# Seven-product column pairs in the branch gates and the output projection, with a group's late work spread over the next group and operands made chunk by chunk

## The chip, the cores and the metric

The kernel runs on one core of a Trainium2 chip. The metric is the device time of one execution in microseconds (us), given as the median of several runs. All data are float32; a weight or an activation is split into a rounded float32r part ("high") and the remainder ("low"), and a product is made of three matmuls: high times high, low times high, high times low.

## The reference, cut to what matters

One layer of a hybrid block for 256 rows of width 4096. Every matrix product below has 256 rows on the left.

```
xn   = rms_norm(x, norm_in_g)
proj = xn @ w_in                      # 4096 -> q, k, v, z_a, a_c, g_c, z_c, each 2048 wide
y_a  = rms_norm(attention(q, k, v), attn_out_g) * silu(z_a)
y_c  = rms_norm(conv_module(a_c, g_c), conv_out_g) * silu(z_c)
h    = x + concat(y_a, y_c) @ w_out   # 4096 x 4096
gate = sigmoid(rms_norm(h, ple_norm_g) @ w_ple_gate + b_ple_gate)   # 4096 x 4096
h    = h + gate * (p @ w_ple)         # 256 x 4096
out  = rms_norm(h, final_g)
```

The norms' row factors are applied after the products; their column gains go into the left operand.

## The kernel before, in words

**Left operands.** A 256 x 512 chunk of activations is turned by TensorE (`transposed`, L142: eight transposes of 128 x 128) and split into high and low (`split_from_psum`, L132: ScalarE writes the high part at L136, VectorE the low part at L137) into one tile `big_t` for four contraction blocks of 128. The operands of the products are `xT` (of x, eight tiles), `yT` (of the gated branches) and `hT` (of h).

**Plain products.** `product` (L206) makes 256 x 512 results: for each pair of contraction blocks it loads a 512 KB weight tile `wt` on SyncE's queue, ScalarE casts it to `wh` (L188), VectorE makes the remainder `wl` (L189), and TensorE does 12 matmuls (2 blocks x 2 row halves x 3 kinds) into two PSUM banks. A full chunk of 512 columns has 192 matmuls. After each weight tile `fill(2)` takes two pieces of postponed work from the list `later`.

**Seven-product units.** `mixed_product` (L276) makes 256 x 1024 results. One unit is two contraction blocks, that is 2 x 2 blocks of the left operand and 2 x 2 of the weights. A plain unit does the eight block products, 24 matmuls. A starred unit does seven (a Strassen-Winograd scheme), 21 matmuls: it needs four sums of left blocks, made once by `combine` (L253, tiles `hS`) and two sum tiles of weights, `ua` and `ub`, which VectorE makes for each unit in four additions of 512 columns (L330 to L335). In a starred unit VectorE makes two remainders of 1024 columns for `ua` and `ub`, one of 1024 for the second weight tile and one of 512 for the first, beside these four additions; in a plain unit it makes two remainders of 1024. A starred unit uses four more PSUM banks, the helpers `P1`, `P5`, `P6`, `P7`, which share the pool of the transposes. The order of the 16 units of a group is a string; a star marks a seven-product unit. The groups of before have 7 starred and 9 plain units, 7 x 21 + 9 x 24 = 363 matmuls in place of 384.

**The stages after attention**, in the order of the work:

- the convolution's pointwise product (`w_pw`, L710);
- the branch gates: `gated` (L721), eight plain chunks of `w_in`; after each chunk silu on ScalarE (L725) and one multiplication for each row half on VectorE (L726), then `to_operand` (the chunks of the attention at once, those of the convolution after the last gate);
- the output projection (L751): eight plain chunks of `w_out`; after each, the residual sum (L758), the square sums (L759), the operand `hT` and its sums `hS` for one pair of blocks in four;
- the embedding gates (L850): chunks 0 to 5 of `w_ple_gate` as three groups of `mixed_product`, here called E1, E2, E3. `add_gated_pair` (L813) follows each group: the sums of the helpers (L820 to L828), two small products with `w_ple`, and for each of four quarters the last sum (L837), the sigmoid (L838), three VectorE steps (L839, L840, L842) and a square sum on ScalarE (L841);
- chunks 6 and 7 as plain products, then the final norm.

**What sets the order.** A scheduler arranges each engine's instructions from the program's order; each engine then works through its list strictly in that order, and so do SyncE's DMA issues. Pools bound how far an engine can run ahead: five weight tiles `wt`, three each of `wh` and `wl`, two each of `uh` and `ul`, four PSUM banks for results and four for transposes or helpers.

Of the kernel before, what the change touches and what calls it, by code (L numbers as in the profile page):

```python
# [26 lines left out]
def hybrid_block(  # L27
# [113 lines left out]

    def transposed(src, blocks, then=lambda ins: None):  # L142

        pt = tmp_psum()
        for i, b in enumerate(blocks):
            for h in range(NH):
                then(
                    nc.tensor.transpose(  # L148
                        pt[:, i * T + h * P : i * T + (h + 1) * P],
                        src[:, h, b * P : (b + 1) * P],  # L150
                        ident,
                    )
                )
        return [pt[:, i * T : (i + 1) * T] for i in range(len(blocks))]
# [51 lines left out]
    def product(w, col, lhs, kblocks, pool=None, tag="acc", ahead=None, lag=(), given=()):  # L206
# [9 lines left out]
        for k0 in starts:  # L216
# [18 lines left out]
            fill(2)  # L235
# [17 lines left out]
    def combine(dst, at, pts, g):  # L253
# [9 lines left out]
        stt(s5, pts[1][:, P:], g[:, 1:2], a10, ALU.mult, ALU.subtract)  # L263
        stt(s2, s5, -1.0, a00, ALU.mult, ALU.subtract)
        stt(s4, pts[1][:, :P], g[:, 1:2], s2, ALU.mult, ALU.add)
# [3 lines left out]
        nc.vector.tensor_tensor(lo, src, hi.bitcast(F32), ALU.subtract)  # L269

# [5 lines left out]
    def mixed_product(w, col, lhs, comb, order, after=None):  # L276
# [25 lines left out]

        for n, (pair, seven) in enumerate(order):
            wts = []
# [16 lines left out]
            if not helper:  # L321
# [17 lines left out]
            def s_of(i):  # L339
                t, at = comb(pair)  # L340
# [378 lines left out]


    def gated(y, col, r_y):  # L721
        acc = product(w_in0, col, xT, KD)
        sz = spool.tile([P, NH, NB], F32, tag="stage", name="sz")
        for h in range(NH):
            nc.scalar.activation(sz[:, h, :], acc[h], AF.Silu, scale=r_x[:, h : h + 1])  # L725
            nc.vector.scalar_tensor_tensor(  # L726
                y[:, h, :], y[:, h, :], r_y[:, h : h + 1], sz[:, h, :], ALU.mult, ALU.mult
            )

    def to_operand(y, g, c):  # L730
# [3 lines left out]
    yT = []
    for c, y in enumerate(y_a):
        gated(y, o_za + c * NB, r_a)
        to_operand(y, ga, c)
    for c, y in enumerate(y_c):
        gated(y, o_zc + c * NB, r_c)
    for c, y in enumerate(y_c):  # L740
        to_operand(y, gc, c)


    hs, hT, hS = [], [], []
    last_transpose = []

    def hT_last(ins):
        last_transpose[:] = [ins]

    ssq_h = cpool.tile([P, NH, D // NB], F32, name="ssq_h")  # L750
    for c in range(D // NB):  # L751
        hc = act.tile([P, NH, NB], F32, tag="act", name="hc")
        nc.sync.dma_start(
            hc, x[0, :, c * NB : (c + 1) * NB].rearrange("(h q) n -> q h n", q=P)
        )
        acc = product(w_out[0], c * NB, yT, KD)
        for h in range(NH):
            nc.vector.tensor_tensor(hc[:, h, :], acc[h], hc[:, h, :], ALU.add)  # L758
            square_sum(ssq_h[:, h, c : c + 1], hc[:, h, :])  # L759
        t = big_tile()  # L760
        if c % 2 == 0:
            hS.append(big_tile())
        for pair in range(2):
            blocks = (2 * pair, 2 * pair + 1)
            pts = transposed(hc, blocks, then=hT_last)
            for b, pt in zip(blocks, pts):
                split_from_psum(t, b, pt, gp[:, 4 * c + b : 4 * c + b + 1])
            if pair == 0 and c < D // NB - 1:
                combine(hS[c // 2], 2 * (c % 2), pts, gp[:, 4 * c : 4 * c + 2])
        hs.append(hc)  # L770
        hT.append(t)
# [3 lines left out]
    pin = spool.tile([P, NH, PLE], F32, tag="stage", name="pin")  # L775
    nc.sync.dma_start(pin, p[0, 0].rearrange("(h q) n -> q h n", q=P))
    pT = spool.tile([P, PLE // P, 2, T], F32R, tag="pT_in", name="pT_in", bufs=1)
    ppt = tmp_psum()
    for b in range(PLE // P):
        for h in range(NH):  # L780
            nc.tensor.transpose(
                ppt[:, b * T + h * P : b * T + (h + 1) * P], pin[:, h, b * P : (b + 1) * P], ident
            )
        split_from_psum(pT, b, ppt[:, b * T : (b + 1) * T], 1.0)
# [28 lines left out]
    def add_gated_pair(c0, c, helper):  # L813
# [97 lines left out]
```

## Time and profile before

| | us |
|---|---|
| median of the 3 runs shown | 2111.97 (2111.31 to 2112.86) |
| the profiled execution, whole | 2111.11 |
| its span, first to last instruction | 2109.1 |
| TensorE busy (matmuls) | 2086.6 |
| VectorE busy | 1388.8 |
| ScalarE busy | 999.3 |
| GpSimd busy | 37.6 |
| mean granted TensorE clock | 0.997 |

The profiled execution took 2.0 us more than its span and 0.9 us less than the median. Matmuls are pipelined: each is shown for 0.39 us but the next begins after 0.23 us, so a busy share says when TensorE had something to do, and the number of matmuls in a stretch says how fast it went. An idle time in brackets stands ahead of an instruction with what released it. Stretches of a window view can be cut at any time; here they are cut at the first matmul of a group.

### The profile page before, as it was taken

What the parts mean: (1) busy time and instruction counts of PE and PEld (TensorE: products, weight loads), DVE (VectorE), ACT (ScalarE), POOL (GpSimd) and SP (SyncE); (2) the same over time, 40 slices, a digit from 0 to 9 for tenths busy, and PEclk for the clock granted to TensorE, in tenths of its full rate; (3) what the DMA queues carried; (4) which work ended last, traced back from release to release, by engine and by line L of the source; (5) the groups of instructions that cost most, each with busy time, mean ns of one, the idle gap of its engine ahead of it and who ended that gap; (6) DMA issues with size and microseconds to landing.
All of it is one profiled execution on the core that took longest, in us unless ns stands there. A gap on an engine that the chain in (4) does not pass through costs nothing.

```text
span 2109.1 us, 25226 instructions
## 1 busy us (share of the span) xinstructions
PE 2086.6 (99%) x9386; PEld 1717.3 (81%) x9386; DVE 1388.8 (66%) x1817; ACT 999.3 (47%) x1256; POOL 37.6 (2%) x38
## 2 busy tenths in 40 slices
PE   9999999999999999999999999999999999999997
PEld 7888888888888888888888888888888888787886
DVE  5599965498548956765455444465544479999854
ACT  7444445444544444654444444454444465555544
POOL 0000000000000002200000000000000000000000
PEclk9999999999999999999999999999999999999999
DMA  8666666666666665656666666676666666666664
GB/s 287 189 190 190 189 191 179 191 188 190 180 190 189 190 199 162 187 173 208 193 200 206 200 191 196 197 219 189 190 190 190 191 195 202 198 215 213 210 206 168
DMA packets 203092, 412.23 MB, mean 195 GB/s; under 512 B 13006, under 2 KB 16222, under 8 KB 202970
## 3 DMA queue, kind: packets, MB, share of 16 engines
q1 hardware_dynamic: 202682, 410.11, 63.9%
q8 instruction: 73, 1.20, 0.2%
q10 hardware_dynamic: 288, 0.52, 0.1%
q14 instruction: 49, 0.40, 0.1%
HBM read 406.39 MB, written 4.19 MB: 195 GB/s over the span
## 4 chain that ended last, share of the span: by engine, by line
PE 96%; DVE 2%; DMA 1%; issue 1%; ACT 0%; POOL 0%; SPq 0%; ACTq 0%; POOLq 0%; DVEq 0%
PE acc L201 82%; PE acc L292 9%; PE acc_P L292 3%; PE tmp_ps L148 1%; DMA xin<-in_x_dram 1%; DVE wl L189 1%; PE tmp_ps L616 0%; PE tmp_ps L631 0%; PE tmp_ps L649 0%; DVE z L839 0%; DMA wt<-in_w_ple_gate_dram 0%; PE tmp_ps L655 0%; PE tmp_ps L656 0%; PE tmp_ps L630 0%; ACT wh L188 0%
## 5 line engine op out<-in xcount | busy, mean ns | idle before, releaser
L201 PE MATMUL acc<-wh,big_t 128*128 128x512 f32 x5088 | 1585.9, 392 | 0.1
L189 DVE TENSOR_TENSOR wl<-wt,wh 128x1024 fp32r<-128x1024 f32 (+1 forms) x741 | 901.7, 1220 | 628.0 <-ACT wh L188 625.4
L188 ACT CAST wh<-wt 128x1024 fp32r<-128x1024 f32 (+1 forms) x741 | 768.2, 1039 | 961.4 <-PE acc L201 855.7
L201 PEld LDWEIGHTS acc<-wh,big_t 128*128 128x128 f32 x5088 | 954.3, 188 | 195.0 <-DVE big_t L137 0.7
L201 PE MATMUL acc<-wl,big_t 128*128 128x512 f32 x2544 | 992.3, 390 | 0.6 <-DVE wl L189 0.5
L201 PEld LDWEIGHTS acc<-wl,big_t 128*128 128x128 f32 x2544 | 478.2, 188 | 99.3 <-DVE wl L189 1.7
L467 DVE SCALAR_TENSOR_TENSOR cv<-uT,dw,cv 128x256 f32<-128x256 f32 x480 | 202.1, 478 | 0.5
L292 PE MATMUL acc<-wh,big_t 128*128 128x512 f32 x516 | 158.9, 391 | 0.0
L292 PEld LDWEIGHTS acc<-wh,big_t 128*128 128x128 f32 x516 | 97.3, 189 | 20.8 <-ACT wh L188 0.4
L292 PE MATMUL acc<-wl,big_t 128*128 128x512 f32 x258 | 98.7, 394 | 3.6 <-DVE wl L189 3.6
L292 PEld LDWEIGHTS acc<-wl,big_t 128*128 128x128 f32 x258 | 48.7, 190 | 14.5 <-DVE wl L189 4.4
L292 PE MATMUL acc_P<-uh,big_t 128*128 128x512 f32 x126 | 38.5, 391 | 0.0
L188 ACT CAST uh<-ub 128x1024 fp32r<-128x1024 f32 x21 | 22.1, 1052 | 29.1 <-DVE ub L335 23.9
L137 DVE SCALAR_TENSOR_TENSOR big_t<-tmp_ps,prm,big_t 128x256 fp32r<-128x256 f32 x64 | 27.8, 477 | 2.6 <-ACT big_t L136 2.4
L136 ACT ACTIVATE big_t<-tmp_ps,prm 128x256 fp32r<-128x256 f32 x64 | 26.9, 471 | 5.4 <-DVE big_t L137 5.3
L292 PEld LDWEIGHTS acc_P<-uh,big_t 128*128 128x128 f32 x126 | 23.3, 188 | 5.6 <-ACT uh L188 1.1
L189 DVE TENSOR_TENSOR ul<-ub,uh 128x1024 fp32r<-128x1024 f32 x21 | 25.6, 1219 | 3.5 <-ACT uh L188 3.5
L188 ACT CAST uh<-ua 128x1024 fp32r<-128x1024 f32 x21 | 22.1, 1051 | 10.9 <-DVE ua L331 10.2
L189 DVE TENSOR_TENSOR ul<-ua,uh 128x1024 fp32r<-128x1024 f32 x21 | 25.6, 1219 | 1.5 <-ACT uh L188 1.5
L362 ACT ACTIVATE junk<-hc 128x512 bf16<-128x512 f32 x32 | 19.9, 623 | 11.1 <-DVE hc L840 6.0
L292 PE MATMUL acc_P<-ul,big_t 128*128 128x512 f32 x63 | 24.0, 392 | 0.0
L330 DVE TENSOR_TENSOR ua<-wt 128x512 f32<-128x512 f32 x21 | 14.4, 688 | 12.1 <-DMA wt<-in_w_ple_gate_dram 12.0
(176 smaller groups left out, 766.3 us busy)
## 6 DMA issues: line engine op xcount, KB each, us to landing
wt<-in_w_in_dram SPq DMA_DIRECT2D x447, 512.0 KB, 3.9
wt<-in_w_out_dram SPq DMA_DIRECT2D x128, 512.0 KB, 3.7
wt<-in_w_ple_gate_dram SPq DMA_DIRECT2D x128, 512.0 KB, 4.1
wt<-in_w_pw_dram SPq DMA_DIRECT2D x32, 512.0 KB, 4.5
hc<-in_x_dram SPq DMA_DIRECT2D x8, 512.0 KB, 4.9
wt<-in_w_ple_dram SPq DMA_DIRECT2D x8, 512.0 KB, 4.9
out_dram<-hc SPq DMA_DIRECT2D x16, 256.0 KB, 2.9
xin<-in_x_dram SPq DMA_DIRECT2D x7, 512.0 KB, 8.4
```

Of the source, the lines that this page charges most:

```text
L136: nc.scalar.activation(hi, src, AF.Identity, scale=scale),
L137: nc.vector.scalar_tensor_tensor(lo, src, scale, hi.bitcast(F32), ALU.mult, ALU.subtract),
L148: nc.tensor.transpose(pt[:, i * T + h * P : i * T + (h + 1) * P], src[:, h, b * P : (b + 1) * P], ident,)
L188: nc.scalar.copy(wh[:, :kc, :], wt[:, :kc, :]),
L189: nc.vector.tensor_tensor(wl[:, :kc, :], wt[:, :kc, :], wh[:, :kc, :].bitcast(F32), ALU.subtract),
L201: nc.tensor.matmul(acc, a, b[:, k, :], start=kb == 0 and kind == 0, stop=kb == kblocks - 1 and kind == 2,)
L292: nc.tensor.matmul(banks[name], a, b, start=name not in begun, stop=final and ends[name] == n and kind == 2,)
L330: plus(ua[:, 0], w0[:, 0], w0[:, 1])
L362: nc.scalar.activation(junk, src, AF.Square, accum_out=dst)
L467: nc.vector.scalar_tensor_tensor(cv[:, i, :], uT[:, i, k : k + T], dw[:, b, k : k + 1], cv[:, i, :], ALU.mult, ALU.add,)
```

## The change

- The branch gates become four groups of `mixed_product` (here G1 to G4), the output projection four groups (W1 to W4). The embedding gates keep three groups (E1 to E3) and two plain chunks.
- Three orders replace two: `steady` (7 starred units) for most groups, `delayed` (5) for G1, `late` (4) for W1 and E1. Before, E1 had 7. Starred units: G 5 + 7 + 7 + 7, W 4 + 7 + 7 + 7, E 4 + 7 + 7, in all 69 against 21.
- The sums of left blocks for x (`xS`) are made from the split operand (`combine_again`); those for y and h by `combine` as before.
- `operand` makes an operand chunk with its sums; `y_ahead` and `h_ahead` call it from within W1 and E1, two chunks before the first unit and one more as the units go on, so that the operands of y and of h are made inside the first group that uses them.
- The sums of the helpers run right after the last starred unit (`on_helpers`). After a group only the four last sums and the activation are left at once; the rest (`later`) is taken two pieces per unit (four in the embedding gates) during the next group.

The core of the diff:

```diff
-    def mixed_product(w, col, lhs, comb, order, after=None):
+    steady = units("1 0* 3 2* 5 4* 7 6* 9 8* 11 10* 13 12* 15 14")
+    delayed = units("1 3 5 7 0* 9 2* 11 4* 13 6* 15 8* 10 12 14")
+    late = units("1 3 5 7 9 11 13 15 0* 2 4* 6 8* 10* 12 14")
+
+    def mixed_product(w, col, lhs, comb, order, on_helpers, ahead=None, fills=0, on_begin=None):
...
+        last_seven = max(n for n, (_, seven) in enumerate(order) if seven)
         for n, (pair, seven) in enumerate(order):
+            if ahead:
+                ahead(pair)
...
+                fill(fills)
                 continue
...
+            if n == last_seven:
+                on_helpers(helper)
+            fill(fills)
+        return c
...
+    def operand(src, g, c, tiles, combs):
+        t = big_tile()
+        if c % 2 == 0:
+            comb_tile(combs)
+        for pair in range(2):
+            blocks = (2 * pair, 2 * pair + 1)
+            pts = transposed(src, blocks)
+            for b, pt in zip(blocks, pts):
+                split_from_psum(t, b, pt, g[:, b : b + 1])
+            if pair == 0 and c < D // NB - 1:
+                combine(combs[c // 2], 2 * (c % 2), pts, g[:, :2])
+        tiles.append(t)
...
-    def gated(y, col, r_y):
-        acc = product(w_in0, col, xT, KD)
...
+    def helper_sums(helper, z):
+        z01, z10, z11 = z[0][:, 1], z[1][:, 0], z[1][:, 1]
+        nc.scalar.copy(z10, helper["P1"])
+        tt(z10, helper["P6"], z10, ALU.add)
+        tt(z01, helper["P5"], z10, ALU.add)
+        tt(z10, helper["P7"], z10, ALU.add)
+        tt(z11, helper["P5"], z10, ALU.add)
...
+    def gated(ys, c0, col, r_y, order):
+        z = sum_tiles()
+        def on_helpers(helper):
+            nc.scalar.copy(z[0][:, 0], helper["P1"])
+            helper_sums(helper, z)
+        acc = mixed_product(w_in0, col + c0 * NB, xT, xS, order, on_helpers, fills=2)
+        for h, j in ((0, 0), (1, 0), (0, 1), (1, 1)):
+            zz, y = z[h][:, j], ys[c0 + j][:, h, :]
+            tt(zz, acc[h][j], zz, ALU.subtract if j else ALU.add)
+            nc.scalar.activation(zz, zz, AF.Silu, scale=r_x[:, h : h + 1])
+            later.append(partial(stt, y, y, r_y[:, h : h + 1], zz, ALU.mult, ALU.mult))
...
-        acc = product(w_out[0], c * NB, yT, KD)
...
+        acc = mixed_product(
+            w_out[0], c0 * NB, yT, yS, steady if c0 else late, on_helpers,
+            ahead=None if c0 else y_ahead, fills=2,
+        )
+        for h, j in ((0, 0), (1, 0), (0, 1), (1, 1)):
+            hc = hs[c0 + j][:, h, :]
+            tt(hc, acc[h][j], hc, ALU.add)
+            later.append(partial(square_sum, ssq_h[:, h, c0 + j : c0 + j + 1], hc))
...
+    def gated_pair(c0, order, ahead):
...
+        todo = []
+        for h, j in ((0, 0), (1, 0), (0, 1), (1, 1)):
+            gt, hc = z[h][:, j], hs[c0 + j][:, h, :]
+            stt(gt, acc[h][j], r_h[:, h : h + 1], gt, ALU.mult, ALU.subtract if j else ALU.add)
+            nc.scalar.activation(gt, gt, AF.Sigmoid)
+            later.append(partial(tt, gt, pacc[j][h], gt, ALU.mult))
+            todo.append(partial(tt, hc, hc, gt, ALU.add))
+            todo.append(partial(square_sum, ssq_f[:, h, c0 + j : c0 + j + 1], hc))
+            todo.append(partial(tt, hc, hc, fgs[j], ALU.mult))
+        later.extend(todo)
```

How instructions move, at three places that the prediction speaks of.

VectorE, from E1 to E2, before: L837 are the four last sums, L839, L840 and L842 the late steps, `wl_13930` and `wl_13946` the remainders of E2's first unit.

```order
L837 SCALAR_TENSOR_TENSOR z_13839<-acc11_13176,r_h_13156,z_13839 128x512
L839 TENSOR_TENSOR z_13838<-acc0_13849,z_13838 128x512
L839 TENSOR_TENSOR z_13839<-acc1_13850,z_13839 128x512
L840 TENSOR_TENSOR hc_10553<-hc_10553,z_13838 128x512
L840 TENSOR_TENSOR hc_10553<-hc_10553,z_13839 128x512
L839 TENSOR_TENSOR z_13838<-acc0_13869,z_13838 128x512
L842 TENSOR_TENSOR hc_10553<-hc_10553,row_13889 128x512 x2
L840 TENSOR_TENSOR hc_10880<-hc_10880,z_13838 128x512
L839 TENSOR_TENSOR z_13839<-acc1_13870,z_13839 128x512
L189 TENSOR_TENSOR wl_13930<-wt_13925,wh_13929 128x1024
```

The same place in the change: L933 are the last sums, L171 the late steps taken from the list, `wl_14689` and `wl_14705` E2's first unit.

```order
L933 SCALAR_TENSOR_TENSOR z_13754<-acc11_13758,r_h_13748,z_13754 128x512
L192 TENSOR_TENSOR wl_14689<-wt_14684,wh_14688 128x1024
L171 TENSOR_TENSOR z_13753<-acc0_14630,z_13753 128x512
L171 TENSOR_TENSOR z_13754<-acc1_14631,z_13754 128x512
L383 TENSOR_TENSOR ua_14732<-wt_14724,wt_14726 128x512
L171 TENSOR_TENSOR z_13753<-acc0_14650,z_13753 128x512
L192 TENSOR_TENSOR wl_14705<-wt_14686,wh_14704 128x1024
L171 TENSOR_TENSOR z_13754<-acc1_14651,z_13754 128x512
L192 TENSOR_TENSOR wl_14735<-wt_14724,wh_14734 128x512
```

The first remainder of E2 stood behind nine late steps and now stands right behind the last sums, and only four late steps are left ahead of the first starred unit's remainders.

VectorE, from G2 to G3, in the change: `wl_9454` and `wl_9470` are G3's first unit, L809 the last sums of G2, L171 its late multiplications.

```order
L192 TENSOR_TENSOR wl_9454<-wt_9449,wh_9453 128x1024
L192 TENSOR_TENSOR ul_9504<-ua_9495,uh_9503 128x1024
L809 TENSOR_TENSOR z_8762<-acc00_8764,z_8762 128x512
L809 TENSOR_TENSOR z_8763<-acc10_8766,z_8763 128x512
L809 TENSOR_TENSOR z_8762<-acc01_8765,z_8762 128x512
L809 TENSOR_TENSOR z_8763<-acc11_8767,z_8763 128x512
L192 TENSOR_TENSOR wl_9470<-wt_9451,wh_9469 128x1024
L171 SCALAR_TENSOR_TENSOR y_a_6141<-y_a_6141,r_a_7401,z_8762 128x512
```

Before, two plain chunks met here, with two multiplications between remainders:

```order
L189 TENSOR_TENSOR wl_8691<-wt_8688,wh_8690 128x1024
L726 SCALAR_TENSOR_TENSOR y_a_4380<-y_a_4380,r_a_7401,sz_8644 128x512
L189 TENSOR_TENSOR wl_8709<-wt_8706,wh_8708 128x1024
L726 SCALAR_TENSOR_TENSOR y_a_4380<-y_a_4380,r_a_7401,sz_8644 128x512
L189 TENSOR_TENSOR wl_8727<-wt_8724,wh_8726 128x1024
```

The four last sums stand in one row ahead of the second remainder of the next group's first unit.

The start of W1 in the change, on TensorE: the last matmuls of G4 (into `acc11`), the transposes of two y chunks, the first matmuls of W1 on blocks of `big_t_10818`.

```order
L339 MATMUL acc11_10129<-wl_10782,big_t_528 128x512
L150 MATMUL tmp_ps_10820<-ident_96,y_a_2607 128x128 x4
L150 MATMUL tmp_ps_10838<-ident_96,y_a_2607 128x128 x4
L150 MATMUL tmp_ps_10848<-ident_96,y_a_4380 128x128 x4
L150 MATMUL tmp_ps_10866<-ident_96,y_a_4380 128x128 x4
L339 MATMUL acc00_10814<-wh_10879,big_t_10818 128x512
```

and on ScalarE, where L810 are G4's silus, L191 a cast of W1's weights, L136 the high parts of the first operand:

```order
L810 ACTIVATE z_10124<-z_10124,r_x_613 128x512
L191 CAST wh_10944<-wt_10940 128x1024
L810 ACTIVATE z_10125<-z_10125,r_x_613 128x512
L810 ACTIVATE z_10124<-z_10124,r_x_613 128x512
L810 ACTIVATE z_10125<-z_10125,r_x_613 128x512
L136 ACTIVATE big_t_10818<-tmp_ps_10820,prm_619 128x256
L136 ACTIVATE big_t_10818<-tmp_ps_10838,prm_619 128x256
```

The first operand of W1 comes right after G4's last matmul on TensorE, and behind a cast and three silus on ScalarE. Before, the chunks of the attention were turned between the gates, and plain matmuls stood between those of the convolution.

More of the change, by code (lines that the diff above doesn't have):

```diff
@@ L204, in accumulate, with product @@
             )
[L206 removed]
+    def product(w, col, lhs, kblocks, pool=None, tag="acc", ahead=None, lag=(), given=(), fills=2):
         acc = [
@@ L350, in mixed_product @@
             add("P4", block(k1, 1), (ubh[:, 1], ubl[:, 1]), n, True)
-            if after is not None and len(begun) and first >= 0 and not getattr(add, "tied", False):
+            if begins and on_begin:
+                on_begin()
+            if begins:
                 tc.add_manual_dep(
-                    made[first].ins, after.ins.name,
+                    made[first].ins, last_transpose[0].ins.name,
                     mybir.DependencyInfo(mybir.DependencyClass.NoSync, mybir.DependencyReason.DATA),
-                    reason="transposes before helpers",
+                    reason="transposes before the helpers take their banks",
                 )
-                add.tied = True
-        return c, helper
+            if n == last_seven:
+                on_helpers(helper)
+            fill(fills)
+        return c
     def square_sum(dst, src):
@@ L734, in hybrid_block @@
[L734 to L754, printed above, removed]
-        )
-        acc = product(w_out[0], c * NB, yT, KD)
[L757 to L771, printed above, removed]
@@ L772, in hybrid_block @@
-    r_h = rstd_of(ssq_h, D, "r_h")
[L775 to L784, printed above, removed]
+    tt, stt = nc.vector.tensor_tensor, nc.vector.scalar_tensor_tensor
@@ new lines, in helper_sums, with sum_tiles @@
+    def helper_sums(helper, z):
[5 more added lines that the diff above has]
+        tt(z11, helper["P5"], z10, ALU.add)
+    def sum_tiles():
+        return [spool.tile([P, 2, NB], F32, tag="stage", name="z") for _ in range(NH)]
+    xS = []
+    for c in range(D // NB - 1):
+        if c % 2 == 0:
+            comb_tile(xS)
+        combine_again(xS[c // 2], 2 * (c % 2), xT[c], 0)
@@ new lines, in hybrid_block, with y_ahead @@
+    for ys, o_z, r_y in ((y_a, o_za, r_a), (y_c, o_zc, r_c)):
+        for c0 in range(0, len(ys), 2):
+            gated(ys, c0, o_z, r_y, delayed if ys is y_a and c0 == 0 else steady)
+    fill(len(later))
+    yT, yS = [], []
+    def y_ahead(pair):
+        while len(yT) < min(pair // 2 + 2, D // NB):
+            c = len(yT)
+            y, g, at = (y_a[c], ga, 4 * c) if c < len(y_a) else (y_c[c - len(y_a)], gc, 4 * (c - len(y_a)))
+            operand(y, g[:, at : at + 4], c, yT, yS)
+    hs, hT, hS = [], [], []
@@ new lines, in hybrid_block, with embedding, h_ahead @@
+    fill(len(later))
+    r_h = rstd_of(ssq_h, D, "r_h")
+    pT = []
+    def embedding():
+        pin = spool.tile([P, NH, PLE], F32, tag="row", name="pin", bufs=3)
+        nc.sync.dma_start(pin, p[0, 0].rearrange("(h q) n -> q h n", q=P))
+        pT.append(hS[-1][:, 2:, :, :])
+        for b, pt in enumerate(transposed(pin, range(PLE // P))):
+            split_from_psum(pT[0], b, pt, 1.0)
+    def h_ahead(pair):
+        while len(hT) < min(pair // 2 + 2, D // NB):
+            c = len(hT)
+            operand(hs[c], gp[:, 4 * c : 4 * c + 4], c, hT, hS)
+            if len(hT) == D // NB:
+                embedding()
@@ L859, in hybrid_block @@
+        later.extend(todo)
+    for c0 in range(0, n_f - 2, 2):
+        gated_pair(c0, steady if c0 else late, None if c0 else h_ahead)
     for c in range(n_f - 2, n_f):
```

121 lines of the change are left out of this document (64 added, 57 removed).

## The prediction

> **What bounds the kernel now.** I read the page first, then a table of stretches, then the order of time around the slowest of them. The page's span, busy times and chain of waits:
>
> ```profile
> span 2109.1 us, 25226 instructions
> ...
> PE 2086.6 (99%) x9386; PEld 1717.3 (81%) x9386; DVE 1388.8 (66%) x1817; ACT 999.3 (47%) x1256; POOL 37.6 (2%) x38
> ...
> PE 96%; DVE 2%; DMA 1%; issue 1%; ACT 0%; POOL 0%; SPq 0%; ACTq 0%; POOLq 0%; DVEq 0%
> ```
>
> TensorE holds 96% of the chain, so a matmul removed is worth its full distance to the next one, as long as the other engines keep up. The long merged pieces of the chain give that distance, and the time of a transpose:
>
> ```profile
> 1198.93 171.41 PE acc L201 x756
> ...
> 1730.82 0.82 PE tmp_ps L148 x6
> ```
>
> 171.41 / 756 = 0.2267 us for a matmul. Next, stretches cut at the first matmul of a gate chunk, an output chunk, E1, E2, E3 and chunk 6, then a steady piece inside E2, then the start of E2. The columns are length, then busy time and count of each engine, then the clock.
>
> ```profile
> 1016.40:1059.90 43.50, 43.50 (x194) 36.03 (x193) 21.24 (x21) 18.75 (x21) 0.69 (x1) 1.00 0.66 194
> 1419.20:1462.70 43.50, 43.50 (x195) 35.79 (x193) 23.53 (x27) 19.48 (x24) 0.00 (x0) 1.00 0.64 188
> 1729.46:1818.58 89.12, 89.12 (x400) 73.62 (x399) 79.71 (x100) 52.87 (x63) 0.69 (x1) 1.00 0.64 204
> 1818.58:1912.22 93.64, 90.30 (x388) 73.21 (x387) 86.00 (x105) 52.78 (x66) 0.00 (x0) 0.98 0.62 203
> 1912.22:2004.88 92.66, 91.22 (x400) 74.39 (x399) 86.50 (x105) 52.09 (x64) 0.00 (x0) 1.00 0.65 210
> 2004.88:2049.38 44.50, 43.98 (x193) 35.88 (x192) 24.42 (x23) 18.12 (x21) 0.00 (x0) 1.00 0.71 213
> 1856.00:1876.40 20.40, 20.40 (x92) 16.89 (x91) 18.73 (x22) 12.27 (x13) 0.00 (x0) 1.00 0.63 200
> ...
> 1821.50:1826.50 5.00, 2.61 (x7) 1.79 (x8) 5.00 (x8) 2.61 (x6) 0.00 (x0) 0.80 0.28 87
> 1826.50:1830.00 3.50, 3.50 (x14) 2.81 (x13) 3.50 (x6) 0.20 (x2) 0.00 (x0) 0.80 0.81 269
> ```
>
> A plain chunk takes 43.50 us, 192 x 0.2267 = 43.53: TensorE never waits, and VectorE is busy for half of it. E1 and E2 have 363 + 24 = 387 matmuls, 87.7 us; E3's stretch has 12 more, 90.5 us. So E1 loses 89.12 - 87.7 - 0.82 (six transposes) = 0.6 us, E2 5.9, E3 2.2, chunk 6 1.0: 9.7 us together. All of it lies where one group meets the next. TensorE there, and VectorE in the same time:
>
> ```profile
> 1821.76 0.73 PE L292 MATMUL acc_P<-wh,big_t 128*128 128x512 f32 x2 [1.21 <-ACT wh L188]
> ...
> 1824.62 2.07 PE L292 MATMUL acc<-wl,big_t 128*128 128x512 f32 x4 [2.13 <-DVE wl L189]
> ```
>
> ```profile
> 1815.32 2.72 DVE L837 SCALAR_TENSOR_TENSOR z<-acc,r_h,z 128x512 f32<-128x512 f32 x4
> ...
> 1823.36 1.21 DVE L189 TENSOR_TENSOR wl<-wt,wh 128x1024 fp32r<-128x1024 f32 x1
> ```
>
> E2's first remainder comes at 1823.36, after sixteen pieces of late work that began at 1815.32.
>
> **Part 1: fewer matmuls.** 69 starred units against 21, three matmuls each: 144 fewer, 144 x 0.2267 = -32.65 us, all on the path. The transposes stay 64 for y and 64 for h.
>
> **Part 2: VectorE has to keep up.** Its instructions overlap a little. In the steady piece of E2:
>
> ```profile
> 1864.85 0.68 DVE L189 TENSOR_TENSOR wl<-wt,wh 128x512 fp32r<-128x512 f32 x1
> 1865.45 0.68 DVE L334 TENSOR_TENSOR ub<-ua,wt 128x512 f32<-128x512 f32 x1
> 1866.06 1.22 DVE L189 TENSOR_TENSOR ul<-ua,uh 128x1024 fp32r<-128x1024 f32 x1
> 1867.20 0.68 DVE L335 TENSOR_TENSOR ub<-ub,wt 128x512 f32<-128x512 f32 x1
> ```
>
> From start to start an operation of 512 columns takes 0.605 us and one of 1024 takes 1.14; a four-operand step takes about 0.67 (2.72 us hold four). A plain unit then needs 2 x 1.14 = 2.28 us, a starred one 3 x 1.14 + 5 x 0.605 = 6.45, the pair 8.7 us beside 45 x 0.2267 = 10.2 us of TensorE. The steady piece holds two pairs in 20.40 us without a gap on TensorE. A group of 7 and 9 units: 9 x 2.28 + 7 x 6.45 = 65.7 us.
>
> - G2 to G4: 65.7 + 8 sums (4.8) + 4 late steps (2.7) = 73 us, beside 363 x 0.2267 = 82.3.
> - W2 to W4: 65.7 + 12 x 0.605 = 73 us, beside 82.3.
> - E2, E3: 65.7 + 8 x 0.67 + 16 x 0.605 + 2 x 1.14 = 83 us (the row of E2 says 86.0), beside 87.7. This is nearly full.
> - W1, E1: the operands come in addition.
>
> What one operand costs VectorE and ScalarE, and the other ScalarE steps that the starts need, from the page and the sums' own view:
>
> ```profile
> L188 ACT CAST wh<-wt 128x1024 fp32r<-128x1024 f32 (+1 forms) x741 | 768.2, 1039 | 961.4 <-PE acc L201 855.7
> ...
> L137 DVE SCALAR_TENSOR_TENSOR big_t<-tmp_ps,prm,big_t 128x256 fp32r<-128x256 f32 x64 | 27.8, 477 | 2.6 <-ACT big_t L136 2.4
> L136 ACT ACTIVATE big_t<-tmp_ps,prm 128x256 fp32r<-128x256 f32 x64 | 26.9, 471 | 5.4 <-DVE big_t L137 5.3
> ...
> L362 ACT ACTIVATE junk<-hc 128x512 bf16<-128x512 f32 x32 | 19.9, 623 | 11.1 <-DVE hc L840 6.0 <-DVE hc L796 3.0 <-POOL hc L796 2.1
> ```
>
> ```profile
> L262 DVE TENSOR_TENSOR s_comb<-a_comb x7: 284/286/289, 1423.5 to 1726.1; 128x128 f32<-128x128 f32 x7
> ...
> L265 DVE SCALAR_TENSOR_TENSOR s_comb<-tmp_ps,prm,s_comb x7: 339/351/351, 1424.4 to 1727.0; 128x128 f32<-128x128 f32 x7
> L269 DVE TENSOR_TENSOR big_t<-s_comb,big_t x7: 681/684/686, 1426.1 to 1728.8; 128x512 fp32r<-128x512 f32 x7
> ```
>
> 32 low parts of 0.48 and seven sums of four small steps (0.29 to 0.35) and one of 0.68 are at most 29 us, overlapped about 24. W1 needs 12 x 2.28 + 4 x 6.45 = 53.2, + 24 to 29, + 12 x 0.605 + 4 x 0.67 = 87 to 92 us, beside 372 x 0.2267 + 64 x 0.137 (a transpose, 0.82 / 6) = 93 us of TensorE; E1 needs 88 to 93 beside 99. TensorE stays the longer one, narrowly. For moments in which it doesn't I add 1 us, with 0 to 6 as ends. The sums for x cost VectorE some 17 us beside `w_pw` and G1, where it is half idle: nothing; without that cover they would delay G1 by as much.
>
> SyncE's queue: in W1 the eight loads of h's residual stand between the weights, each waiting until a chunk of y has been turned. Five weight tiles cover two and a half units, 13 us, and TensorE turns each chunk one to two units ahead: nothing; without the cover, a few us once. GpSimd's list is unchanged.
>
> **Part 3: late work spread.** Of the 9.7 us I leave 2 for E2 and E3, where VectorE is nearly full (ends 0 and 9.7): -7.7 us. What is late next is VectorE's last sums, which wait for the group's last matmul and hold up the second remainder of the next first unit. From G2 to G3 four sums and one remainder end about 0.2 + 0.6 + 1.14 = 2 us after the last matmul; TensorE asks for it after 12 matmuls, 2.7 us. That fits by 0.7 us. For the eight starts in G and W without operands to make (G1 to G4, W2 to W4, and the hand-over to E1's weights) I take 0.3 us each, +2.4 (ends: 0 as in the steady piece, 5.9 as in E2).
>
> **Part 4: two starts with no operand ready.** W1 and E1 open with 16 transposes and then need the high part of blocks 2 and 3. On ScalarE stand ahead of it, both times, a cast that waits for the last group's buffer (1.04 us), three silus (an estimate: as long as a square sum, 0.62) or three square sums (0.62 and a read-out), and two high parts (0.47). That is some 3.7 to 4.1 us, of which the transposes cover 1.7 (from 1370.19 to 1371.85 below):
>
> ```profile
> 1370.19 1.91 PE L148 MATMUL tmp_ps<-ident,y_c 128*128 128x128 f32 x16
> 1371.85 0.70 PE L201 MATMUL acc<-wh,big_t 128*128 128x512 f32 x2
> ```
>
> I take 2.0 us at W1 and 2.3 at E1, +4.3 (ends 0, had matmuls been at hand as here, and 5.3). After E2's waits of 1.21 and 2.13 us the clock was 0.80 for 8.5 us, 1.7 us lost; after waits of this size I count half of it for each start, +1.7 (ends 0 and 3.4).
>
> The Trainium skill, page "TensorE: Matmul & The Clock Gate", says in "Part 4: PE-mode transpose" that transposes do not count as busy for the gate, and in "Why this matters for your kernels" that idle gaps over about 3 us bring the slow clock back. By it the transposes would join both waits to gaps of about 4 us, and an estimate from the page's window of 3.4 us at half rate is 1.7 us for each start, so the sum below would end 1.7 us higher. The trace agrees that waits lower the clock, but the sixteen transposes above were followed by matmuls at full distance.
>
> **Sum.** -32.65 - 7.7 + 2.4 + 4.3 + 1.7 + 1.0 = -30.95 us. On the profiled execution 2111.1 becomes 2080.2; the median of before is 0.9 higher, so 2081.
>
> **Rivals.**
>
> - *VectorE becomes the bound.* If its instructions didn't overlap, at 1.22 and 0.68 us as shown, W1 would need 98 us for 93, E1 99 for 99, E2 and E3 91 for 88 each. That is +4 in place of the 1 us above, +4.6 in place of the 2, and with no slack left the eight boundaries cost 1 us and not 0.3, +5.6: 2095. For it: E2 and E3 are 98% full. Against: E2's stretch shows 86.0 and not 91.
> - *Every wait goes.* All 9.7 us return, the new starts cost nothing: 2112.0 - 32.65 - 9.7 = 2069.6. For it: E1 before lost only 0.6 us, with seven starred units. Against: the cast ahead of the silus at W1 can't begin before G4 ends.
> - *Each new boundary costs what E2's did.* The last sums stand in VectorE's list ahead of the next group's second remainder; if they hold it up as the late work did, eight new boundaries x 5.9 = +47.2 us, against -32.65: 2126.5, slower. The point from which it decides is 32.65 / 8 = 4.1 us for a boundary. For it: E2. Against: four sums stand there, not sixteen steps.
> - *The gain doesn't appear.* The removed matmuls were hidden behind something else, or the scheduler's order runs against itself (remainders behind steps that wait): 2112. Against: plain chunks take exactly their matmuls.
>
> **How the numbers follow.** Forecast 0.60, VectorE 0.17, every wait gone 0.15, boundaries 0.05, no gain 0.03. The range runs from the third case to the second, 2069 to 2095, and leaves 0.08 out. A change of 0.2% (4 us) is about what the measurement can tell from none: faster 0.92, same 0.03, slower 0.05.
>
> **What would show it.** Right: 144 fewer matmuls of 512 columns; G2 to G4 and W2 to W4 at 82 to 83 us from first matmul to first matmul; waits of 2 to 3 us on TensorE at the starts of W1 and E1, ended by ScalarE's high parts; E2 and E3 at 88 to 89 us. Wrong: G or W groups of 86 us and more with VectorE busy throughout; waits ended by `wl` in every group; a clock under 0.98 in many stretches; SyncE waiting on `hc` with VectorE waiting on weights.

## The result and the profile after

The changed kernel takes 2077.59 us (median of 4 runs, 2073.5 to 2077.91) where the kernel before takes 2111.82 (4 runs): a ratio of 0.9833, 95% interval 0.9816 to 0.985. It is 34.2 us faster; the forecast was 2081, with a range from 2069 to 2095. The profiled execution took 2077.91 us, so it stands 33.2 us under the profiled 2111.1 of before.

The page of the changed kernel, with its span, busy times and chain:

```profile
span 2075.9 us, 25611 instructions
...
PE 2053.2 (99%) x9242; PEld 1691.1 (81%) x9242; DVE 1638.5 (79%) x2246; ACT 1087.0 (52%) x1385; POOL 39.8 (2%) x38
...
PE 95%; DVE 2%; DMA 1%; issue 1%; ACT 1%; POOL 0%; SPq 0%; ACTq 0%; POOLq 0%; DVEq 0%
```

TensorE has 9386 - 9242 = 144 matmuls fewer, VectorE 249.7 us more to do, and the chain is still TensorE's. All waits of TensorE from 1000 us on, by who ended them (us in total, times, longest):

```profile
PE acc L339 <- ACT big_t L136: 3.5, 2, 1.8
PE acc L339 <- DVE wl L192: 0.6, 1, 0.6
PE acc L339 <- DVE z L809: 0.4, 2, 0.3
PE acc L339 <- DVE big_t L137: 0.4, 1, 0.4
```

That is 5.0 us. The two waits on `z` are G1 to G2 and G2 to G3 (0.28 and 0.17 us): TensorE waits for the last sums themselves, which read the banks that the next group writes. No other steady boundary, and none in the embedding gates, has any. The rest belongs to W1 and E1. In TensorE's order of time both starts look alike:

```profile
1349.43 1.91 PE L150 MATMUL tmp_ps<-ident,y_a 128*128 128x128 f32 x16
...
1353.11 1.21 PE L339 MATMUL acc<-wh,big_t 128*128 128x512 f32 x4 [1.77 <-ACT big_t L136]
1354.69 0.80 PE L339 MATMUL acc<-wh,big_t 128*128 128x512 f32 x1 [0.37 <-DVE big_t L137]
...
1358.05 0.86 PE L339 MATMUL acc<-wh,big_t 128*128 128x512 f32 x3
...
1694.27 1.91 PE L150 MATMUL tmp_ps<-ident,hc 128*128 128x128 f32 x16
...
1697.95 1.43 PE L339 MATMUL acc<-wh,big_t 128*128 128x512 f32 x5 [1.77 <-ACT big_t L136]
```

Sixteen transposes, then 1.77 us for ScalarE's high part. ScalarE's list at W1 is the one that the prediction gave, a cast, three silus and two high parts:

```profile
1349.44 1.05 ACT L191 CAST wh<-wt 128x1024 fp32r<-128x1024 f32 x1 [0.41 <-PE acc L339]
1350.39 1.94 ACT L810 ACTIVATE z<-z,r_x 128x512 f32<-128x512 f32 x3
1352.24 0.81 ACT L136 ACTIVATE big_t<-tmp_ps,prm 128x256 fp32r<-128x256 f32 x2
```

The 0.37 us behind it are a wait for VectorE's low part, which stands behind four late multiplications of G4 (1351.12 to 1353.77). At W1 the matmuls from 1354.69 to 1358.05 stand 0.42 us apart on average and not 0.23: eight took 3.36 us where 1.81 would do, 1.55 lost. The table of stretches shows the clock there, and beside it the start of E1, a group of the branch gates, and the stretches of E2 and E3:

```profile
1353.10:1358.00 4.90, 4.52 (x12) 3.36 (x13) 4.65 (x11) 1.34 (x3) 0.00 (x0) 0.65 0.69 233
1698.00:1702.00 4.00, 4.00 (x18) 3.31 (x19) 2.79 (x10) 2.63 (x5) 0.69 (x1) 1.00 0.41 136
...
1101.69:1183.79 82.10, 81.93 (x361) 67.54 (x361) 73.45 (x86) 48.09 (x53) 0.00 (x0) 1.00 0.62 200
...
1792.00:1885.00 93.00, 93.00 (x411) 76.68 (x410) 88.58 (x108) 53.72 (x67) 0.00 (x0) 1.00 0.65 215
1885.00:1975.00 90.00, 90.00 (x398) 74.10 (x397) 85.16 (x102) 53.37 (x66) 0.00 (x0) 1.00 0.66 216
```

G2 takes 82.10 us, with VectorE busy 73.45 of them. In the embedding gates VectorE is busy for 95% and TensorE still doesn't wait. How long a group is can also be read from the chain of work: the same unbroken piece comes back in each group (start, length, matmuls):

```profile
1434.65 17.02 PE acc L339 x75
1517.82 17.00 PE acc L339 x75
1600.42 17.00 PE acc L339 x75
...
1777.19 11.56 PE acc L339 x51
1865.14 11.56 PE acc L339 x51
1953.11 11.56 PE acc L339 x51
```

The output groups repeat after 83.17 and 82.60 us, for 363 x 0.2267 = 82.3; the embedding groups after 87.95 and 87.97, for 387 x 0.2267 = 87.7. Before, E2's and E3's stretches lost 5.9 and 2.2 us. What became of VectorE's list at E2's start:

```profile
1788.13 2.72 DVE L933 SCALAR_TENSOR_TENSOR z<-acc,r_h,z 128x512 f32<-128x512 f32 x4
...
1790.77 1.21 DVE L192 TENSOR_TENSOR wl<-wt,wh 128x1024 fp32r<-128x1024 f32 x1
...
1791.90 1.28 DVE L171 TENSOR_TENSOR z<-acc,z 128x512 f32<-128x512 f32 x2
...
1794.30 1.22 DVE L192 TENSOR_TENSOR wl<-wt,wh 128x1024 fp32r<-128x1024 f32 x1
```

The next remainder comes 2.6 us after the last sums began, and late work (L171) stands between remainders. Before, it came 8.0 us after them.

### The profile page after: what moved, and what is told of

Its sections match the earlier page's. It is cut to its first block, busy times and chain, and to the rows that moved or that the text cites. A ratio compares the mean times of both kernels' runs of the same rounds, so it can differ in the third digit from the quotient of the medians.

```text
span 2075.9 us, 25611 instructions
## 1 busy us (share of the span) xinstructions
PE 2053.2 (99%) x9242; PEld 1691.1 (81%) x9242; DVE 1638.5 (79%) x2246; ACT 1087.0 (52%) x1385; POOL 39.8 (2%) x38
## 4 chain that ended last, share of the span: by engine, by line
PE 95%; DVE 2%; DMA 1%; issue 1%; ACT 1%; POOL 0%; SPq 0%; ACTq 0%; POOLq 0%; DVEq 0%
PE acc L204 50%; PE acc L339 33%; PE acc_P L339 9%; DVE wl L192 1%; PE tmp_ps L150 1%; DMA wt<-in_w_in_dram 0%; PE tmp_ps L672 0%; PE tmp_ps L687 0%; PE tmp_ps L705 0%; DMA xin<-in_x_dram 0%; DMA wt<-in_w_out_dram 0%; ACT wh L191 0%; DVE z L809 0%; PE tmp_ps L711 0%; PE tmp_ps L712 0%
## 5 line engine op out<-in xcount | busy, mean ns | idle before, releaser
L191 ACT CAST wh<-wt 128x1024 fp32r<-128x1024 f32 (+1 forms) x741 | 742.9, 1011 | 751.6 <-PE acc L204 499.4
L204 PE MATMUL acc<-wh,big_t 128*128 128x512 f32 x3040 | 951.0, 392 | 0.6 <-ACT big_t L136 0.3
L204 PEld LDWEIGHTS acc<-wh,big_t 128*128 128x128 f32 x3040 | 569.9, 188 | 117.0 <-ACT big_t L136 1.0
L339 PE MATMUL acc<-wh,big_t 128*128 128x512 f32 x1972 | 610.3, 391 | 4.4 <-ACT big_t L136 3.5
L204 PE MATMUL acc<-wl,big_t 128*128 128x512 f32 x1520 | 593.0, 390 | 0.1
L339 PEld LDWEIGHTS acc<-wh,big_t 128*128 128x128 f32 x1972 | 369.6, 188 | 82.3 <-ACT big_t L136 4.0
L339 PE MATMUL acc<-wl,big_t 128*128 128x512 f32 x986 | 384.5, 391 | 1.0 <-DVE wl L192 0.6
L204 PEld LDWEIGHTS acc<-wl,big_t 128*128 128x128 f32 x1520 | 285.8, 188 | 58.4 <-DVE wl L192 0.5
L339 PEld LDWEIGHTS acc<-wl,big_t 128*128 128x128 f32 x986 | 185.7, 188 | 42.4 <-DVE wl L192 3.7
L191 ACT CAST uh<-ub 128x1024 fp32r<-128x1024 f32 x69 | 72.6, 1052 | 84.8 <-DVE ub L387 68.1
L339 PE MATMUL acc_P<-uh,big_t 128*128 128x512 f32 x366 | 112.1, 389 | 0.0
L191 ACT CAST uh<-ua 128x1024 fp32r<-128x1024 f32 x69 | 72.7, 1054 | 45.1 <-DVE ua L383 43.7
L192 DVE TENSOR_TENSOR ul<-ub,uh 128x1024 fp32r<-128x1024 f32 x69 | 84.2, 1221 | 14.9 <-ACT uh L191 14.6
L192 DVE TENSOR_TENSOR ul<-ua,uh 128x1024 fp32r<-128x1024 f32 x69 | 84.1, 1219 | 0.0
L382 DVE TENSOR_TENSOR ua<-wt 128x512 f32<-128x512 f32 x69 | 47.5, 689 | 40.7 <-DMA wt<-in_w_in_dram 18.6
L383 DVE TENSOR_TENSOR ua<-wt 128x512 f32<-128x512 f32 x69 | 47.3, 685 | 1.9 <-DMA wt<-in_w_in_dram 1.7
```

Source lines behind the costliest of these rows:

```text
L191: nc.scalar.copy(wh[:, :kc, :], wt[:, :kc, :]),
L192: nc.vector.tensor_tensor(wl[:, :kc, :], wt[:, :kc, :], wh[:, :kc, :].bitcast(F32), ALU.subtract),
L204: nc.tensor.matmul(acc, a, b[:, k, :], start=kb == 0 and kind == 0, stop=kb == kblocks - 1 and kind == 2,)
L339: nc.tensor.matmul(banks[name], a, b, start=name not in begun, stop=final and ends[name] == n and kind == 2,)
L382: plus(ua[:, 0], w0[:, 0], w0[:, 1])
L383: plus(ua[:, 1], w0[:, 1], w1[:, 1])
```

## The experiments

The theory: the gain is the matmuls (-32.65 us) and the waits that spreading takes out of the embedding gates; what it gives back lies at the starts of W1 and E1; VectorE keeps up with some 9 us to spare in each steady group. Two rivals: spreading isn't what took the waits away, and VectorE already bounds the groups. The times below are medians of 4 or 5 runs each; the changed kernel is the measure. Run again beside three of the kernels (late work at once in the embedding gates, seven starred units, both first chunks early), it gave 2077.47 us (2075.87 to 2079.47):

> The changed kernel unaltered, as the measure for the other kernels run beside it on the same chip. Every theory expects 2077.6 us, as in three of its four runs so far; the fourth gave 2073.5, and a second run near 2073.5 would say that a difference of 4 us between two kernels must rest on several runs.

It stayed near 2077.6. The other kernels ran in two further sets without it. The kernel before, which ran in every set, gave 2111.2, 2110.6 and 2112.3 us, so a comparison across sets carries about 1 us more. Differences of 2 us are at the edge of what these runs resolve.

**Embedding gates changed alone.** The kernel before, with the changed `gated_pair` (spread late work, helper sums at the last starred unit) and before's count of starred units, 21:

```diff
-        add_gated_pair(
-            c0,
-            *mixed_product(
-                w_ple_gate[0], c0 * NB, hT, lambda pair: (hS[pair // 4], pair % 4),
-                order if c0 else first_order, None if c0 else last_transpose[0],
-            ),
-        )
+        gated_pair(c0, order if c0 else first_order, None)
```

> The kernel before, with its plain branch gates and plain output projection, and with the changed embedding gates alone: late work spread two steps per unit, helper sums made at the last seven-product unit. The first of its groups makes seven of its eight units in seven products, as before, so the count of matmuls stays that of the kernel before. Theory: of the kernel's gain of 33 to 34 us, the waits of 9.7 us in the embedding gates are the only part that isn't matmuls; here they go and nothing else changes: 8 to 9.7 us less than before, 2101.5 to 2103.5. Rival: the waits went because W4 before them is now spread too and VectorE enters the embedding gates with less behind it; then this kernel keeps them, 0 to 2 us less, 2110.

Measured: 2102.93 us against 2110.56 beside it, a ratio of 0.9964 (0.9951 to 0.9977): 7.6 us less, and 8.2 between the profiled spans (2109.1 and 2100.9). Its list of TensorE's waits from 1000 us on is empty. The page and the chain:

```profile
PE 2083.7 (99%) x9386; PEld 1716.5 (82%) x9386; DVE 1388.6 (66%) x1817; ACT 999.2 (48%) x1256; POOL 37.6 (2%) x38
...
1890.09 11.56 PE acc L293 x51
1978.13 11.56 PE acc L293 x51
```

As many matmuls as before, and embedding groups 88.0 us apart. The rival falls: this needs nothing of the output projection. (This expectation and the next speak of two steps per unit; in the embedding gates it is four.)

From here to the changed kernel it is 25.0 us between the spans: -32.65 for 144 matmuls, + 5.0 of waits, + 1.55 of slow clock, + 1.2 by which W2 and W3 exceed 82.3 (83.17 and 82.60) makes -24.9 (smaller pieces on both sides cancel). The matmuls are worth what they were counted at.

**Late work at once in the embedding gates.** The opposite step, on the changed kernel:

```diff
         later.extend(todo)
+        fill(len(later))
```

> In the embedding gates alone, the late work of a group (its closing sums, copies and sigmoids) is issued in one piece behind the first unit of the next group, as before the change, and not two steps per unit; the helper sums stay where the change has them. Theory: the second remainder of the first unit of E2, E3 and chunk 6 then again stands behind 12 late steps on VectorE, and the 1.2, 2.1, 1.4 and 0.5 us waits that the kernel before showed there come back in part: 4 to 8 us slower than the changed kernel, 2082 to 2086. Rival: the waits were taken away by the helper sums that are made earlier and by the mixed order of units, not by the spreading: 0, within 0.5 us of the changed kernel.

Measured: 2085.88 us, 8.4 more than the changed kernel beside it. The chain, and two rows of TensorE's waits:

```profile
1777.24 11.41 PE acc L339 x50
1868.15 11.56 PE acc L339 x51
1958.24 11.35 PE acc L339 x50
```

```profile
PE acc L339 <- DVE wl L192: 4.6, 7, 1.7
...
PE acc L204 <- DVE wl L192: 2.6, 1, 2.6
```

The groups grow from 87.95 and 87.97 us to 90.9 and 90.1, and chunk 6 begins with a wait of 2.6 us on a remainder, with a slow clock behind it. What the changed embedding gates give alone (7.6) and what the loss of spreading costs (8.4) agree.

**The helper sums last as well.** In addition, `on_helpers` is called behind the group's last unit:

```diff
-            if n == last_seven:
+            if n == last_seven and not sums_last:
                 on_helpers(helper)
...
+        if sums_last:
+            on_helpers(helper)
```

> The changed kernel with the embedding gates' late work in one piece behind the next group's first unit, as in the run of that kind, and their helper sums made behind the group's last unit, as before the change, and not at its last seven-product unit. Theory (the prediction's: the last sums and the late steps both hold up the second remainder of the next group's first unit): 1 to 3 us slower than with the late work alone, 2087 to 2089. Rival: the late work alone makes the waits; the place of the helper sums is worth nothing, 2085.9 within 1 us.

Measured: 2085.25 us, 0.6 under the run before it. The rival is right and the theory's 1 to 3 us aren't there: late steps make the waits, and the place of the helper sums is worth nothing that these runs can tell.

**Late work at once everywhere.** `fill(len(later))` after each group of the branch gates and the output projection too.

> The changed kernel with the late work of every group (branch gates, output projection, embedding gates) issued in one piece behind the first unit of the next group. Theory: in the branch gates and the output projection a group ends on starred units too, so the second remainder of the next group's first units stands behind the late steps on VectorE, as in the embedding gates; with 2 to 4 us for each of the seven boundaries G1 to W1 and W1 to E1, and the 8.4 us that the embedding gates alone gave, 22 to 36 us slower than the changed kernel, 2100 to 2114. Rival: the weights of two more units are loaded ahead, and the branch gates have 8.7 us more of VectorE to spare than the embedding gates; then only those 8.4 us show, 2086.

Measured: 2085.68 us, what the embedding gates alone gave. My theory was wrong by 14 to 28 us: spreading is worth nothing that can be seen in G and W. In G four postponed multiplications then stand ahead of the next remainder, and VectorE has 8.7 us of a group to spare; in W the postponed step is a square sum on ScalarE, and VectorE has none. TensorE's waits on a remainder come to 4.4 us here and to 4.6 with the embedding gates alone. Whether the small number of steps or the spare time makes the difference to the embedding gates was not tried apart.

**More work for VectorE.** One or three additions of 512 columns more for each starred unit of G2 to G4 and W2 to W4, into a tile that nobody reads:

```diff
+            for _ in range(extra):
+                more = spool.tile([P, NB], mybir.dt.bfloat16, tag="junk", name="more")
+                some = lhs[0][:, 0, :, :].bitcast(F32)
+                nc.vector.tensor_tensor(more.rearrange("q (i t) -> q i t", t=T), some, some, ALU.add)
```

`some` is the first block of the left operand, there from the start. In the third kernel, with three additions, the inputs are the unit's own sums `ub[:, 0]` and `ub[:, 1]`.

> The changed kernel with one addition of 512 columns more on VectorE (into a tile that nobody reads) in each of the seven-product units of G2 to G4 and W2 to W4: 7 per group, at 0.605 us apart 4.2 us. Theory: VectorE is busy 73.5 us of a group's 82.1 and has room for it: 0 to 1 us slower, 2077.5 to 2078.6. Rival: VectorE bounds these groups already (the idle time of 8.7 us is forced by what it waits for from ScalarE and the loads): six groups by 4.2, 25 us slower, 2103.

> As the run with one addition more, but with three of them in each seven-product unit: 21 per group, 12.7 us. Theory: 73.5 and 12.7 are 86.2 us of VectorE in a group whose matmuls take 82.1: it becomes the bound and each of six groups grows by 4.1 or more, since its share of work is not even within a group: 24 to 35 us slower than the changed kernel, 2101 to 2113. Rival of a VectorE that bounds already: 76 us slower, 2153. Rival of a bound that is elsewhere however much VectorE has: under 5 us, 2082.

> As the run with three additions more in each seven-product unit of G2 to G4 and W2 to W4, but each addition now reads the unit's own sums of weights, so that it can't be made ahead of its unit; there they read an operand that exists from the start, and 25 of 126 ran in G1's time. Theory: VectorE's room must be counted over as long a stretch as its work can be moved. Tied to their group the 12.7 us meet a room of 8.7 us: 4 us per group, 24 us slower than the changed kernel, 2101, with VectorE busy 98 to 100% of G2 to G4 as well. Rival: the weights are loaded far enough ahead for the work to spread all the same; then it costs the 11.3 us that the untied additions cost, 2089.

Measured: 2079.37, 2088.88 and 2093.22 us: 1.8, 11.3 and 15.6 more. The first 25 us of additions found room almost wholly, but not where they were meant to. With one addition for each unit, G1 has 21 and G2 to G4 have none (a view of the additions alone; the second column is VectorE's time in them and their number):

```profile
1019.00:1102.10 83.10, 13.87 (x21) 1.00 0.62 197
1102.10:1350.50 248.40, 0.00 (x0) 1.00 0.62 204
```

The other 21 ran seven each in W2, W3 and W4, and W2 and W3 still took 82.4 and 82.3 us, as long as their matmuls. So VectorE isn't the bound of W2 and W3; of G2 to G4 this kernel shows nothing. Of 76 us, too, more found room than I had expected (24 to 35 us slower). G1 with three free additions:

```profile
1019.00:1101.70 82.70, 82.35 (x364) 67.90 (x363) 82.52 (x113) 45.74 (x52) 3.81 (x1) 1.00 0.63 202
```

25 of the 126 additions had been put into G1, where no unit asked for one: their operand was ready, and the scheduler filled VectorE's idle time with them. Tied to their units, G1 keeps its idle time and VectorE is full from G2 on:

```profile
1019.00:1101.70 82.70, 82.65 (x364) 67.85 (x363) 70.23 (x88) 46.38 (x51) 3.01 (x1) 1.00 0.63 199
1101.70:1185.00 83.30, 83.30 (x368) 68.45 (x367) 83.30 (x105) 47.39 (x54) 0.00 (x0) 1.00 0.62 201
1185.00:1268.00 83.00, 80.89 (x346) 63.81 (x346) 82.17 (x102) 43.59 (x48) 0.00 (x0) 1.00 0.59 189
```

In G2 VectorE is busy without a pause, and TensorE still doesn't wait, so G2 had the room, too. In the next stretch TensorE makes 346 matmuls, 346 x 0.2267 = 78.4 us of 83.0, and loses the rest. So the theory holds in kind (VectorE is full) and fails in size: 15.6 us and not 24. That VectorE enters G2 and W2 with remainders made ahead would explain the difference and fits G2's row, but I haven't tried it.

**Seven starred units in W1 and E1.** `late` gets three more stars: 18 matmuls fewer.

```diff
-    late = units("1 3 5 7 9 11 13 15 0* 2 4* 6 8* 10* 12 14")
+    late = units("1 3 5 7 9 11 13 15 0* 2* 4* 6* 8* 10* 12* 14")
```

> W1 and E1, the groups that first read a new operand, make seven units in seven products instead of four: 18 matmuls of 512 columns fewer. Theory: VectorE is the bound as soon as a group's additions and remainders exceed its matmuls; by the rows for one unit W1 then asks some 100 to 105 us of VectorE in a group of about 90, and loses 8 to 12 us in W1 and E1 together beside the 4.1 that the matmuls save: 4 to 8 us slower, 2082 to 2086. Rival: VectorE's queue catches up in the next group, since the weights are loaded ahead: 4.1 us faster, 2073.5.

Measured: 2094.72 us, 17.2 more than the changed kernel beside it; with the 4.1 us of matmuls saved, 21.3 us lost. Stretches in W1 and E1, and the wait that heads TensorE's list:

```profile
1420.00:1430.00 10.00, 9.41 (x41) 7.16 (x40) 10.00 (x14) 5.36 (x7) 0.00 (x0) 1.00 0.46 153
1430.00:1440.00 10.00, 7.44 (x32) 5.61 (x31) 10.00 (x13) 6.62 (x8) 0.00 (x0) 1.00 0.55 179
1440.00:1450.00 10.00, 8.37 (x38) 6.59 (x37) 10.00 (x12) 4.82 (x7) 0.00 (x0) 1.00 0.65 220
...
1780.00:1790.00 10.00, 7.47 (x31) 5.29 (x30) 10.00 (x15) 5.98 (x7) 0.00 (x0) 1.00 0.37 119
```

```profile
PE acc_P L339 <- ACT uh L191: 10.0, 10, 1.6
```

VectorE has no pause (10.00 of 10), and TensorE makes 31 to 41 matmuls where 44 fit. The row names ScalarE, yet ScalarE is busy for half to two thirds of the time. Its casts to `uh` stand behind casts that wait for a weight tile, and the loads of weights wait for VectorE. This is the first row of SyncE's own waits from 1405 to 1450 us; the next two name VectorE's `ua` and `wl` (7.2 and 3.4 us):

```profile
SPq L358 <- DVE ub L387: 27.2, 6, 4.8
```

Here VectorE is the bound: four stars fit into W1 and E1, seven don't, and five or six were not tried. The kernel before had seven in E1 and lost 0.6 us there, with nearly all operands of h made in the output projection. The direction was as expected, the net price (17.2 us against 4 to 8) some two to four times as high.

**The first chunk of y and of h made a group earlier.** At the start of G4 the first 512 columns of y are turned and split, at the start of W4 those of h; their sums come from the halves (`combine_again`).

```diff
+            if ys is y_c and c0 == 2:
+                first["y"] = early(y_a[0], ga[:, :4])
...
+        if c0 == D // NB - 2:
+            first["h"] = early(hs[0], gp[:, :4])
```

> The first 512 columns of y are transposed and split at the start of G4, and the first 512 of h at the start of W4, a group ahead of the product that reads them; their sums are then made from the halves, which costs one more addition of 512 columns each. Theory: what W1 and E1 lose at their starts is the way transpose, ScalarE's high part, VectorE's low part, and nothing else; then the 1.77 and 0.37 us ahead of W1, the 1.77 ahead of E1 and the 1.7 us of slow clock behind W1's start all go: 5.6 us less, about 2072 (at least 4 less if the slow clock comes back elsewhere). Rival: the starts are bounded by something later in the chain (the second remainder of the first unit, or the last sums of squares), so the wait only moves to the next matmuls: 0 to 1 us less, 2077. Second rival: the 16 transposes, now in the middle of G4 and W4, hold TensorE there behind temporary banks that the group before still has: 2 to 4 us slower, about 2080.

Measured: 2072.54 us (2072.26 to 2072.69), a ratio of 0.9818 to the kernel before (0.9803 to 0.9832), 4.9 us less than the changed kernel beside it. All its waits on TensorE:

```profile
PE acc L352 <- DVE wl L192: 1.4, 2, 0.9
PE acc_P L352 <- DVE ul L192: 0.6, 1, 0.6
PE acc L352 <- DVE z L822: 0.3, 1, 0.3
```

No wait on `big_t` is left, and no stretch of 4 us between 1000 and 2060 us has a clock under 1.00. The theory's 2072 is what came, and both rivals fall. This kernel is faster than both others: its slowest run lies under every run of the changed kernel (2073.5 and more). Then with y alone, and two of the four rows of its waits:

> The changed kernel with the first 512 columns of y alone made a group ahead; h's first chunk is made at E1's start, as in the changed kernel. Theory: W1's start is worth its waits of 1.77 and 0.37 us and the 1.7 us in which the clock was slow behind them, 3.85 of the 5 us that both starts gave together; E1's wait of 1.77 stays, without a slow clock: 2073.7. Rival: the slow clock is not tied to W1's start, and comes back at E1's or elsewhere: 2.1 us only, 2075.4.

```profile
PE acc L352 <- ACT big_t L136: 1.8, 1, 1.8
PE acc L352 <- DVE wl L192: 1.2, 2, 0.9
```

Measured: 2072.96 us (2071.95 to 2074.14), 4.6 less than the changed kernel. W1's start is worth nearly all, as its waits (1.77, 0.37, and 0.65 further on) and the slow clock (1.55) say: 4.3. E1's wait of 1.77 is still there in this kernel, and its span is 1.4 us longer than with both chunks, but its profiled execution was the slowest of its four; the medians differ by 0.4, which is too little to tell what h's chunk is worth.

## Why the forecast was right, and where it was off

- **Part 1, fewer matmuls: right.** -32.65 us, and the account from the embedding gates alone to the changed kernel closes to 0.1 us with it. The prediction's count of sixteen pieces of late work ahead of E2's first remainder is wrong: the order of instructions shows thirteen, four last sums and nine late steps. Its sum doesn't use the count.
- **Part 2, VectorE keeps up: right, and close.** For G2 it reckoned 73 us beside 82.3; the trace has 73.45 beside 82.10. I added 1 us; TensorE waited 0.65 us for a remainder in W1, and W2 and W3 exceed their matmuls by 1.2. The rival "VectorE becomes the bound" needs 91 us for E2 and E3, which took 88, and 5 us more than its matmuls for W1, which waited 0.65 us for a remainder: it is refuted there. W2 and W3 took seven additions each and G2 took 21 tied ones, without a loss there. It is confirmed for a kernel three stars further in W1 and E1.
- **Part 3, late work spread: right in kind, its boundary term too high.** I returned 7.7 of 9.7 us; alone it returned 7.6 to 8.2. The eight boundaries at 0.3 us came to 0.28 + 0.17 = 0.45 and not 2.4. The step that failed is that the last sums "hold up the second remainder of the next first unit": no boundary in G or W of the changed kernel's profile waited for that remainder, so the 0.7 us by which it fits was enough, and the two waits that came were for the last sums themselves. And with all late work at once G and W lose nothing that can be seen either, so the diff's spreading there is not what keeps those boundaries clear. The rival at 5.9 us a boundary is refuted with it.
- **Part 4, two starts: right.** 4.3 us forecast, 1.77 + 0.37 + 1.77 = 3.9 seen, 3.5 of it behind ScalarE's high parts as said; the 0.37, behind VectorE's late multiplications, was not foreseen. Half a slow clock at each start (1.7) became a whole one at W1 and none at E1 (1.55). That this term came out is luck: the same waits at W1 had no slow clock in two of eight profiles, as the last section shows.

With these the sum is -32.65 + 0.65 + 1.2 - 8.2 + 0.45 + 3.9 + 1.55 = -33.1, against -33.2 between the profiled executions. The 3.4 us by which 2081 is above the median are the boundary term (1.95) with small differences, and 1.2 us between profiled executions and medians on both sides.

## What to carry to other kernels

Where one engine bounds and the next is at 85 to 95%, reckon that next engine group by group, and ask at each boundary which of its steps stand ahead of the one that the bound needs: twelve late steps of VectorE in one piece cost 2 to 3 us a boundary where it was 95% busy, four steps cost nothing that could be seen where it was 89%. A first operand chunk made one group early took the chain of transpose, high part and low part off both starts here for the price of an addition. An experiment that adds work must tie it to the place that it is to load, or a scheduler may put it into idle time elsewhere, as it did here with all 21 additions meant for G2 to G4.

## What the hardware showed

The same gap doesn't always bring the slow clock. In six profiles (the changed kernel twice, all late work at once, the embedding gates as before, one addition more, three free additions) the waits of 1.77 and 0.37 us at W1 lie ahead of 4 us at a mean clock of 0.63 to 0.80. In two (seven starred units; late work at once in the embedding gates) W1 opens with the same waits and keeps a full clock. In the second of these chunk 6, after a wait of 2.58 us, loses it. With all late work at once the same wait at chunk 6 was followed by a full clock, and so was E1's 1.77 us (3.68 with its transposes) in all eight profiles that have it.

Length alone doesn't decide. In the clock records of the thirteen traces each loss behind such a wait is one spell of 3.41 us at half the clock, 1.7 us lost, and the full clock between two slow stretches lasts a whole multiple of 3.413 us (26 to 210 of them). So the clock changes on a fixed beat. Here are one window of that beat and the next, first at W1 in the changed kernel, then at E1 with seven starred units (the clock is the third number from the right; the 17 of E1's window are sixteen transposes and the end of an earlier matmul):

```profile
1350.93:1354.34 3.41, 1.62 (x8) 0.84 (x6) 3.41 (x7) 2.18 (x6) 0.00 (x0) 1.00 0.90 312
1354.34:1357.75 3.41, 3.06 (x7) 2.50 (x8) 3.19 (x8) 1.28 (x3) 0.00 (x0) 0.50 0.58 188
...
1702.74:1706.15 3.41, 1.82 (x17) 1.58 (x15) 3.19 (x6) 3.41 (x9) 0.00 (x0) 1.00 0.49 169
1706.15:1709.56 3.41, 3.23 (x14) 2.70 (x15) 2.89 (x9) 1.95 (x5) 0.69 (x1) 1.00 0.48 154
```

As an estimate, count 0.2267 us for each matmul of 512 columns and 0.104 for each transpose (16 in 1.66 us in the prediction's row). W1's first window is then occupied for 0.33 of its time and E1's for 0.46, all of it by transposes, and only W1 lost the clock behind it. Over all windows of the thirteen traces, the 23 that were occupied for 0.37 or less (13 of them at the end of the kernel) were all followed by a slow stretch, none over 0.40 was, and of the four in between one was. So transposes count as activity here, other than the prediction's reckoning of gaps of about 4 us has it. No kernel was made to test this.

The Trainium skill's page "TensorE: Matmul & The Clock Gate", in "Part 1: The HAM clock gate", says that the activity window runs freely and doesn't start with the kernel; these traces agree, since the first full clock begins 9.5 to 13.4 us behind the first instruction and the beat lies differently from trace to trace. A price for such a gap is therefore, ahead of a run, a chance of up to 1.7 us and not a fixed sum.
